# The last rotary pass of latent attention heads on 32 rows in four row groups, with two key pieces side by side

## The chip, the core and the metric

The kernel runs on one core of one Trainium2 chip. The metric is the time of one execution in device microseconds. Before the change it was 594.4 us (median of three runs, 593.88 to 594.96). Single-precision products are made of matmuls in a rounded single-precision type, three for one exact product: high part by high part, low by high and high by low.

## The reference

One decoder block: 512 tokens and 16 learned leading tokens (528 keys), width 1024. From one projection of the normalised input come two attention branches of 16 heads each. The latent branch (MLA) has queries and keys of 64 plain and 32 rotary features; the rotary key is one for all heads. The other branch (FoX) adds a cumulative forget gate to the scores and has no rotary part.

```python
k_pe = rope(k_pe_raw, pos)[:, None]
q_m = jnp.concatenate([q_nope, rope(q_pe, pos)], axis=-1)
k_m = jnp.concatenate([k_nope, jnp.broadcast_to(k_pe, (B, MLA_HEADS, L, MLA_ROPE_DIM))], axis=-1)
o_mla = causal_block_attention(q_m, k_m, v_mla, MLA_SCALE)
y_mla = (o_mla * jax.nn.silu(z_mla)) @ w_br_mla[l]
...
o_fox = causal_block_attention(fox_heads(fq), fox_heads(fk), fox_heads(fv), FOX_SCALE, cum)
y_fox = (o_fox * jax.nn.silu(z_fox)) @ w_br_fox[l]
mixed = (jax.nn.sigmoid(gate_a) * y_mla + jax.nn.sigmoid(gate_b) * y_fox) @ w_out[l]
h = h + rmsnorm(mixed, post_norm_g[l])
```

## The kernel before

The kernel has a preparation (norm, transposes, latent projections), an attention part of sixteen stages and a merge of the branches. A stage is one branch and one pair of heads; FoX and MLA alternate, so there are eight MLA stages. In the attention part the order of TensorE's instructions is the order of the program text (`manual_schedule`); the other engines and SP's queue of DMAs are ordered by a scheduler. Between the parts of a stage stand "fills": projections for the next stage (`fq`, `fk`, `v`, `z`, `mq`, `mk`) and for gates (`pg`), full 128-row matmuls that need nothing of the running softmax.

A stage begins with `scores(0)`: the query tiles 0, 1 and 2 (128 queries each) against the 144, 272 and 400 keys that they may see. Tile 0 and tile 1 share a PSUM bank, tile 2 has its own; there is one such set for each head of the pair, four banks in all (pool `stp`, names `st`). Then come the products with the values of the stage before (`ov`, function `values`), then `scores(1)`: tile 3 against all 528 keys, in pieces of 272 and 256 keys, in the same four banks again. VectorE takes the scores out of the banks (L783), ScalarE makes the exponentials, and SP turns the probabilities with DMA transposes (`pt<-pn`), which the `ov` products of the next stage read.

Each piece of an MLA stage takes five passes, and each pass two matmuls, one per head, on partitions 0 to 63 and 64 to 127. Such a pair runs side by side in two halves of the array's rows. Three passes are the plain features (`hlk,hlq`). Two are the rotary ones: the tile `QP` holds, for each head, the high part of the rotary query on 32 partitions and its low part on the next 32. `KP[0]` (shown as KPH) holds the high part of the rotary key four times, on each group of 32 partitions, so one pass makes high by high and low by high. `KP[1]` (KPL) holds the key's low part at partitions 0 and 64, and zeros (L231) on the 32 partitions behind each, so the last pass of 64 rows makes high by low. These five are listed in `sets` (L737) and issued in `scores` (L761). A run of three rows in the timeline, hlk, KPH and KPL, is one piece.

`QP` is filled by DMA: for the first pair of heads from SBUF in `rest` (L643), for later pairs from a DRAM tile in `load_qp` (L570). The copies of the rotary key are made once, ahead of the stages (L916 to L918).

Of the kernel before, what the change touches and what calls it, by code (L numbers as in the profile page):

```python
# [23 lines left out]
S = 512  # L24
# [25 lines left out]
def f32(ap):  # L50
    return ap.bitcast(F32)
# [3 lines left out]
def block_kernel(ctx: ExitStack, tc: tile.TileContext, x, meta_tokens, pre_norm_g, w_in, fox_forget_b,  # L55
# [40 lines left out]
    def mm(*a, **k):  # L96
        nc.tensor.matmul(*a, **k)  # L97
# [441 lines left out]
    with ExitStack() as att:  # L539
# [6 lines left out]

        cb = [[thp.tile([128, L], F32, tag="th", name=f"cb{n}{h}") for h in range(2)] for n in "pm"]
        QP = ac.tile([128, S], F32R, tag="QP", name="QP")
        maskt = ac.tile([128, L + 16], BF16, tag="maskt", name="maskt")
        nc.gpsimd.memset(maskt, 0.0)  # L550
        nc.gpsimd.affine_select(out=maskt[:, 400:L], in_=maskt[:, 400:L], pattern=[[-1, 128]], base=0,
# [17 lines left out]

        def load_qp(pr):  # L570
            dma(f32(QP), qpe_dram[2 * pr : 2 * pr + 2].rearrange("h i x f s -> (h i x f) s"))

        def q_mla(pr):
            ld = []
# [30 lines left out]
        def pe_unit(g):  # L605
# [37 lines left out]
            def rest(x):  # L643

                tt, rr = room()[1], results(x)
                with nullcontext() if g else tc.issue_after(masks[0]):
                    nc.gpsimd.tensor_tensor(out=tt[:, x], in0=tt[:, x], in1=tt[:, 3 - x], op=(ALU.subtract, ALU.add)[x])
                hi, lo = rr[:, 0], rr[:, 1]
                nc.gpsimd.tensor_copy(hi.bitcast(F32R), tt[:, x])
                split_lo(nc.gpsimd, lo.bitcast(F32R), tt[:, x], hi)  # L650
                if g:
                    store(x, 0, 8)
                else:

# [75 lines left out]
        def attention(br, pr):  # L730
# [30 lines left out]
            def scores(g):  # L761

                banks = (((0, 0, 144, 0), (1, 0, 272, 144)), ((2, 0, 400, 0),)) if g == 0 else \
                    (((3, 0, HALF, 0),), ((3, HALF, L - HALF, 0),))

                def fn():
# [3 lines left out]
                    sfs[g] = aw.tile([128, 2, (2 * SF_STEP + 400, L)[g]], F32, tag=f"sf{g}", name=f"sf{nm_}{g}", bufs=1)  # L770
                    for ib, parts in enumerate(banks):
                        ps = [stp.tile([128, 512], F32, tag="st", name=f"st{nm_}{g}{ib}{h}") for h in range(2)]
                        for b, c0, w, o in parts:
# [3 lines left out]
                        for b, c0, w, o in parts:  # L777
                            for h in range(2):
                                nb = sums["nb"][:, h, b : b + 1]
                                for a, e, in1 in added(h, b, c0, c0 + w):  # L780

                                    with tc.high_priority(offset=100):
                                        nc.vector.tensor_tensor_reduce(  # L783
                                            out=sf_of(h, b)[:, a:e], in0=ps[h][:, o + a - c0 : o + e - c0],
                                            in1=in1, scale=-scale, scalar=3.0e38 if a == 0 else nb,
                                            op0=ALU.add, op1=ALU.min, accum_out=nb)
# [528 lines left out]
```

## Time and profile before

| | before |
|---|---|
| median of three runs | 594.4 us |
| the profiled execution | 594.59 us |
| its span, first to last instruction | 592.5 us |
| granted TensorE clock, mean | 0.998 |
| TensorE matmul busy | 584.1 us, 3841 matmuls |
| of these, rotary passes of the MLA stages | 160 (80 with KPH, 80 with KPL) |
| VectorE, ScalarE, GpSimd busy | 412.3, 357.8, 200.3 us |

All numbers but the median come from one profiled execution. PE is TensorE's matmuls, PEld its weight loads, DVE VectorE, ACT ScalarE, POOL GpSimd, SPq the queue of SyncE that issues DMAs. A form such as 64*128 64x272 is a matmul with weights of 64 rows by 128 columns and 272 moving columns. In a timeline equal instructions that follow each other stand in one row with a count. Matmuls are pipelined and the ends of their rows are modelled: the distance between starts tells the pace.

### The profile page before, as it was taken

How to read it: one execution, taken by the hardware profiler on the slowest of the kernel's cores; microseconds unless marked ns; L12 is line 12 of the kernel's file. 1: busy time of each engine (PE TensorE's matmuls, PEld its weight loads, DVE VectorE, ACT ScalarE, POOL GpSimd, SP SyncE). 2: the span in 40 equal slices, each digit the busy share in tenths (PEclk: the TensorE clock that was granted, in tenths of full speed). 3: DMA queues.
4: the chain of work that ended last, by engine and by line, in shares of the span. 5: the costliest groups of instructions: out<-in, count | busy, mean ns of one | idle time of the engine just before them, and what ended most of it. 6: DMA issues, size and time to landing. Idle time of an engine off the chain costs nothing.

```text
span 592.5 us, 11129 instructions
## 1 busy us (share of the span) xinstructions
PE 584.1 (99%) x3841; PEld 501.0 (85%) x3841; DVE 412.3 (70%) x1155; ACT 357.8 (60%) x816; POOL 200.3 (34%) x271
## 2 busy tenths in 40 slices
PE   8999999999999999999999999999999999999996
PEld 6989789889889888888898897888998998888884
DVE  5854876775775776766758748797647777468957
ACT  7846775784774784766748748764444363433753
POOL 4317746455358463553544544420000000000000
PEclk9999999999999999999999999999999999999999
DMA  8535599999995998896895986866822534333603
GB/s 288 119 87 161 124 176 239 230 201 225 168 201 116 229 211 217 188 188 175 177 207 147 203 160 146 193 137 216 273 72 71 143 95 132 94 106 108 213 2 142
DMA packets 220001, 97.47 MB, mean 165 GB/s; under 512 B 131457, under 2 KB 209673, under 8 KB 219945
## 3 DMA queue, kind: packets, MB, share of 16 engines
q1 hardware_dynamic: 219944, 96.77, 69.4%
q8 instruction: 30, 0.49, 0.3%
q14 instruction: 27, 0.21, 0.1%
HBM read 62.36 MB, written 3.97 MB: 112 GB/s over the span
## 4 chain that ended last, share of the span: by engine, by line
PE 97%; DMA 1%; SPq 0%; DVE 0%; issue 0%; POOL 0%; DVEq 0%; ACT 0%; POOLq 0%
PE z L97 19%; PE pg L97 15%; PE v L97 9%; PE st L97 8%; PE fk L97 8%; PE fq L97 8%; PE x L97 8%; PE py L97 7%; PE ov L97 5%; PE psm L97 4%; PE y L97 2%; PE mq L97 2%; PE mk L97 1%; DMA wsr<-in_w_in_dram 1%; PE ppe L97 1%; PE pt L100 1%
## 5 line engine op out<-in xcount | busy, mean ns | idle before, releaser
L103 POOL TENSOR_TENSOR wl<-wraw,wh 128x1024 fp32r<-128x1024 f32 (+2 forms) x62 | 120.2, 1947 | 96.3 <-ACT wh L130 73.9
L130 ACT CAST wh<-wraw 128x1024 fp32r<-128x1024 f32 (+1 forms) x72 | 74.6, 1040 | 53.5 <-PE py L97 16.8
L791 ACT ACTIVATE sf<-sf,nb 128x272 f32<-128x272 f32 (+3 forms) x128 | 72.5, 568 | 17.1 <-DVE nb L783 15.6
L819 DVE SCALAR_TENSOR_TENSOR pn<-sf,ri,pn 128x128 f16<-128x128 f32 (+3 forms) x128 | 68.7, 576 | 7.3 <-ACT pn L818 7.1
L103 DVE TENSOR_TENSOR wl<-wraw,wh 128x512 fp32r<-128x512 f32 (+1 forms) x54 | 51.0, 947 | 27.5 <-ACT wh L1052 18.9
L818 ACT ACTIVATE pn<-sf,ri 128x128 f16<-128x128 f32 (+3 forms) x128 | 61.2, 550 | 9.9 <-ACT sf L791 7.9
L97 PE MATMUL z<-uTh,wh 128*128 128x512 f32 x128 | 51.0, 398 | 0.0
L97 PE MATMUL pg<-uTh,wh 128*128 128x512 f32 x128 | 50.3, 393 | 0.0
L97 PE MATMUL z<-uTl,wh 128*128 128x512 f32 x128 | 50.1, 391 | 0.0
L97 PE MATMUL z<-uTh,wl 128*128 128x512 f32 x128 | 50.0, 391 | 0.0
L97 PE MATMUL pg<-uTl,wh 128*128 128x512 f32 x128 | 49.9, 390 | 0.0
L97 PE MATMUL pg<-uTh,wl 128*128 128x512 f32 x128 | 49.9, 390 | 0.0
L97 PE MATMUL st<-hlk,hlq 64*128 64x272 f32 (+3 forms) x480 | 45.5, 308 | 0.0
L1052 ACT CAST wh<-wraw 128x512 fp32r<-128x512 f32 x28 | 17.3, 619 | 39.8 <-DVE wraw L1061 15.4
L687 DVE TENSOR_REDUCE vsc<-v 128x1 f32<-128x272 f32 (+1 forms) x32 | 13.2, 433 | 39.9 <-PE v L97 39.9
L97 PEld LDWEIGHTS st<-hlk,hlq 64*128 64x128 f32 x480 | 34.6, 185 | 6.0 <-ACT vh L706 2.8
L97 PE MATMUL v<-uTh,wl 128*128 128x256 f32 (+1 forms) x128 | 36.5, 285 | 0.0
L97 PE MATMUL fk<-uTl,wh 128*128 128x256 f32 (+1 forms) x128 | 36.5, 285 | 0.0
L97 PE MATMUL fk<-uTh,wh 128*128 128x256 f32 (+1 forms) x128 | 36.5, 285 | 0.0
L97 PE MATMUL v<-uTl,wh 128*128 128x256 f32 (+1 forms) x128 | 36.5, 285 | 0.0
L97 PE MATMUL fk<-uTh,wl 128*128 128x256 f32 (+1 forms) x128 | 36.4, 285 | 0.0
L97 PE MATMUL v<-uTh,wh 128*128 128x256 f32 (+1 forms) x128 | 36.4, 285 | 0.0
(285 smaller groups left out, 1615.4 us busy)
## 6 DMA issues: line engine op xcount, KB each, us to landing
wraw<-in_w_in_dram SPq DMA_DIRECT2D x56, 512.0 KB, 4.5
cbp<-c_dram SPq DMA_DIRECT2D x16, 264.0 KB, 4.5
wraw<-in_w_br_fox_dram SPq DMA_DIRECT2D x8, 512.0 KB, 4.4
tb<-in_w_out_dram SPq DMA_DIRECT2D x8, 512.0 KB, 5.2
wraw<-in_w_br_mla_dram SPq DMA_DIRECT2D x8, 512.0 KB, 4.1
wraw<-in_w_out_dram SPq DMA_DIRECT2D x6, 512.0 KB, 3.6
xr<-in_x_dram SPq DMA_DIRECT2D x4, 512.0 KB
out_dram<-yo SPq DMA_DIRECT2D x8, 256.0 KB, 2.0
```

The source lines that it names most:

```text
L97: nc.tensor.matmul(*a, **k)
L100: nc.tensor.transpose(*a)
L103: return eng.tensor_tensor(out=lo, in0=src, in1=f32(hi), op=ALU.subtract)
L130: nc.scalar.copy(wh[:, :n], raw[:, :n])
L687: nc.vector.tensor_reduce(out=sc[:, i : i + 1], in_=ps, op=ALU.max, axis=AX.X, apply_absolute_value=True)
L791: exps[g] = nc.scalar.activation(sf, sf, AF.Exp, bias=sums["nb"][:, h, b : b + 1], scale=-1.0, accum_out=sums["su"][:, h, b : b + 1]).ins
L818: normed[:] = [nc.scalar.activation(hi, sf, AF.Copy, scale=rib).ins]
L819: nc.vector.scalar_tensor_tensor(out=lo, in0=sf, scalar=rib, in1=hi, op0=ALU.mult, op1=ALU.subtract)
L1052: nc.scalar.copy(to[0], src)
```

## The change

The low rotary pass of the MLA stages uses 32 rows instead of 64: the high part of the rotary query against the low part of the rotary key, without the rows of zeros. The low part of the key is copied to all four groups of 32 partitions. A new tile `Q2` holds the high part of the rotary query a second time, for the upper 256 queries, on the second 32 partitions of each head (partitions 32 to 63 and 96 to 127). With it a second piece of a head can be taken on other rows of the array than the first. The low passes are collected in a list and issued by `own`; the place in the list tells whether a piece reads `QP` or `Q2`. The scores of MLA are evicted once all pieces of a group are complete; FoX is evicted as before.

```diff
+        Q2 = ac.tile([128, S // 2], F32R, tag="Q2", name="Q2")
...
         def load_qp(pr):
             dma(f32(QP), qpe_dram[2 * pr : 2 * pr + 2].rearrange("h i x f s -> (h i x f) s"))
+            for h in range(2):
+                dma(f32(Q2[64 * h + 32 : 64 * h + 64]), qpe_dram[2 * pr + h, 0, :, :, S // 2 :].rearrange("x f s -> (x f) s"))
...
                             dma(f32(QP[r : r + 16]), rr[16 * h : 16 * h + 16, i])
+                        r = 64 * h + 32 + 16 * x
+                        dma(f32(Q2[r : r + 16]), rr[16 * h : 16 * h + 16, 0, S // 2 :])
...
-                return out + [(QP[hs, qs], KP[i][hs, ks]) for i in range(2)]
+                return out + [(QP[hs, qs], KP[0][hs, ks])]
+
+            def low_rotary(h, b, c0, w, moved):
+                rs = slice(64 * h + 32 * moved, 64 * h + 32 * moved + 32)
+                q_ = Q2[rs, 128 * (b - 2) : 128 * (b - 2) + 128] if moved else QP[rs, 128 * b : 128 * b + 128]
+                return q_, KP[1][rs, c0 : c0 + w]
...
-            last_set = (4, 2)[br]
+            last_set = (3, 2)[br]
...
+                def own(late_):
+                    for n, (ps, b, c0, w, o) in enumerate(late_):
+                        for h in range(2):
+                            mm(ps[h][:, o : o + w], *low_rotary(h, b, c0, w, n), start=False, stop=True, skip_group_check=True)
+                    late_.clear()
...
                         for b, c0, w, o in parts:
                             for i, ops in enumerate(zip(*(sets(h, b, c0, w) for h in range(2)))):
                                 for h, (Q, K) in enumerate(ops):
-                                    mm(ps[h][:, o : o + w], Q, K, start=(i == 0), stop=(i == last_set))
...
+                                    mm(ps[h][:, o : o + w], Q, K, start=(i == 0), stop=(br == 1 and i == last_set),
+                                       skip_group_check=not br)
+                            if not br:
+                                late_.append((ps, b, c0, w, o))
+                                if len(late_) == 1 and g == 0:
+                                    own(late_)
+                        if br:
+                            evict(ps, parts)
+                    if not br:
+                        own(late_)
+                        for ps, parts in zip(pss, banks):
+                            evict(ps, parts)
...
-        nc.sync.dma_start(f32(KP[1][64 : 64 + ROPE]), f32(KP[1][0:ROPE]))
+        for r in (64, 32, 96):
+            nc.sync.dma_start(f32(KP[1][r : r + ROPE]), f32(KP[1][0:ROPE]))
```

TensorE, second group of scores (tile 3) of the first MLA stage, before; st_1202 and st_1203 are the banks of the first piece for the two heads, st_1216 and st_1217 those of the second:

```order
L97 MATMUL st_1203<-KPH,QP 128x272
L97 MATMUL st_1202<-KPL,QP 128x272
L97 MATMUL st_1203<-KPL,QP 128x272
L97 MATMUL st_1216<-hlk_1074,hlq_1055 128x256
...
L97 MATMUL st_1217<-KPH,QP 128x256
L97 MATMUL st_1216<-KPL,QP 128x256
L97 MATMUL st_1217<-KPL,QP 128x256
L97 MATMUL fq_1243<-uTh,wh_1237 128x512
```

The same place in the changed program; the four banks are st_1209, st_1210, st_1219 and st_1220, and Q_710 is the tile Q2:

```order
L97 MATMUL st_1210<-KPH,QP 128x272
L97 MATMUL st_1219<-hlk_1081,hlq_1062 128x256
...
L97 MATMUL st_1220<-KPH,QP 128x256
L97 MATMUL st_1209<-KPL,QP 128x272
L97 MATMUL st_1210<-KPL,QP 128x272
L97 MATMUL st_1219<-KPL,Q_710 128x256
L97 MATMUL st_1220<-KPL,Q_710 128x256
L97 MATMUL fq_1250<-uTh,wh_1244 128x512
```

The two KPL rows of the first piece moved behind the second piece and stand beside its own; the number of matmuls is the same.

TensorE, first group (tiles 0, 1, 2) of the same stage in the changed program; 1134 and 1135 are the banks that tiles 0 and 1 share, 1156 and 1157 those of tile 2:

```order
L97 MATMUL st_1135<-KPH,QP 128x144
L97 MATMUL st_1134<-KPL,QP 128x144
L97 MATMUL st_1135<-KPL,QP 128x144
L97 MATMUL st_1134<-hlk_1081,hlq_1062 128x272
...
L97 MATMUL st_1135<-KPH,QP 128x272
L97 MATMUL st_1134<-KPL,QP 128x272
L97 MATMUL st_1135<-KPL,QP 128x272
L97 MATMUL st_1156<-hlk_1081,hlq_1062 128x400
```

Here no row moved: `own` is called after each piece, and each KPL pair, now of 32 rows, stands where it stood before.

SP's queue, DMAs for the first pair of heads, before:

```order
L91 DMA_TRANSPOSE vp_720<-vh 128x9x128
L91 DMA QP<-gT_778 16x512 x4
L91 DMA QP<-gT_779 16x512 x4
L851 DMA cbp_705<-c_dram 128x528
L851 DMA cbp_706<-c_dram 128x528
L91 DMA_TRANSPOSE pt<-pn_715 128x6x128
```

And in the changed program:

```order
L91 DMA_TRANSPOSE vp_721<-vh 128x9x128
L91 DMA QP<-gT_781 16x512 x2
L91 DMA Q_710<-gT_781 16x256
L91 DMA QP<-gT_781 16x512 x2
L91 DMA Q_710<-gT_781 16x256
L91 DMA QP<-gT_782 16x512 x2
L91 DMA Q_710<-gT_782 16x256
L91 DMA QP<-gT_782 16x512 x2
L91 DMA Q_710<-gT_782 16x256
L882 DMA cbp_705<-c_dram 128x528
```

Four small DMAs more stand ahead of the bias loads and of the transposes of the first stage's probabilities.

More of the change, by code (lines that the diff above doesn't have):

```diff
@@ L764, in scores, with evict @@
                     (((3, 0, HALF, 0),), ((3, HALF, L - HALF, 0),))
+                def own(late_):
[3 more added lines that the diff above has]
+                    late_.clear()
+                def evict(ps, parts):
+                    for b, c0, w, o in parts:
+                        for h in range(2):
+                            nb = sums["nb"][:, h, b : b + 1]
+                            for a, e, in1 in added(h, b, c0, c0 + w):
+                                with tc.high_priority(offset=100):
+                                    nc.vector.tensor_tensor_reduce(
+                                        out=sf_of(h, b)[:, a:e], in0=ps[h][:, o + a - c0 : o + e - c0],
+                                        in1=in1, scale=-scale, scalar=3.0e38 if a == 0 else nb,
+                                        op0=ALU.add, op1=ALU.min, accum_out=nb)
                 def fn():
@@ L770, in fn @@
                     sfs[g] = aw.tile([128, 2, (2 * SF_STEP + 400, L)[g]], F32, tag=f"sf{g}", name=f"sf{nm_}{g}", bufs=1)
+                    pss, late_ = [], []
                     for ib, parts in enumerate(banks):
                         ps = [stp.tile([128, 512], F32, tag="st", name=f"st{nm_}{g}{ib}{h}") for h in range(2)]
+                        pss.append(ps)
                         for b, c0, w, o in parts:
@@ L775, in fn @@
                                 for h, (Q, K) in enumerate(ops):
-                                    mm(ps[h][:, o : o + w], Q, K, start=(i == 0), stop=(i == last_set))
[L777 to L786, printed above, removed]
+                                    mm(ps[h][:, o : o + w], Q, K, start=(i == 0), stop=(br == 1 and i == last_set),
[10 more added lines that the diff above has]
+                            evict(ps, parts)
                     with tc.high_priority(offset=60):
```

## The prediction

> **What bounds the kernel now.** I read the page first, then the waits of the matrix engine, then its timeline through one latent stage.
>
> ```profile
> span 592.5 us, 11129 instructions
> PE 584.1 (99%) x3841; PEld 501.0 (85%) x3841; DVE 412.3 (70%) x1155; ACT 357.8 (60%) x816; POOL 200.3 (34%) x271
> PE 97%; DMA 1%; SPq 0%; DVE 0%; issue 0%; POOL 0%; DVEq 0%; ACT 0%; POOLq 0%
> PE spun L97 <- DVE KPL L231: 1.5, 1, 1.5
> PE psm L97 <- POOL wsh L298: 1.1, 1, 1.1
> ```
>
> TensorE (PE) is busy for 99% of the span, the chain that ended last runs over it for 97%, and its only two waits lie before the attention begins. So the order and the spacing of its own matmuls set the time: whatever the latent stages lose or gain there goes into the end one for one, unless a new wait is made. The timeline of the first latent stage, one row for each run of matmuls with one pair of operands, columns start, length, shape, count:
>
> ```profile
> 78.75 0.39 PE L97 MATMUL z<-uTh,wl 128*128 128x512 f32 x1
> 79.07 0.56 PE L97 MATMUL st<-hlk,hlq 64*128 64x144 f32 x6
> 79.47 0.28 PE L97 MATMUL st<-KPH,QP 64*128 64x144 f32 x2
> 79.58 0.28 PE L97 MATMUL st<-KPL,QP 64*128 64x144 f32 x2
> 79.69 0.59 PE L97 MATMUL st<-hlk,hlq 64*128 64x272 f32 x6
> 80.11 0.29 PE L97 MATMUL st<-KPH,QP 64*128 64x272 f32 x2
> 80.24 0.29 PE L97 MATMUL st<-KPL,QP 64*128 64x272 f32 x2
> 80.36 0.71 PE L97 MATMUL st<-hlk,hlq 64*128 64x400 f32 x6
> 80.91 0.34 PE L97 MATMUL st<-KPH,QP 64*128 64x400 f32 x2
> 81.09 0.34 PE L97 MATMUL st<-KPL,QP 64*128 64x400 f32 x2
> 81.37 2.04 PE L97 MATMUL ov<-pt,vp 80*64 80x512 f16 x26
> 83.82 0.29 PE L97 MATMUL st<-KPH,QP 64*128 64x272 f32 x2
> 83.94 0.29 PE L97 MATMUL st<-KPL,QP 64*128 64x272 f32 x2
> 84.07 0.51 PE L97 MATMUL st<-hlk,hlq 64*128 64x256 f32 x6
> 84.42 0.28 PE L97 MATMUL st<-KPH,QP 64*128 64x256 f32 x2
> 84.53 0.28 PE L97 MATMUL st<-KPL,QP 64*128 64x256 f32 x2
> 84.75 0.50 PE L97 MATMUL fq<-uTh,wh 128*128 128x512 f32 x1
> 85.08 0.40 PE L97 MATMUL fq<-uTl,wh 128*128 128x512 f32 x1
> 85.32 0.40 PE L97 MATMUL fq<-uTh,wl 128*128 128x512 f32 x1
> ```
>
> Lengths overlap, so the price of a pair (two heads, x2) is the distance between starts. 144 keys: 79.58 to 79.69, 0.11 us. 272: 80.24 to 80.36, 0.125 (two differences of 0.13 and 0.12). 400: 80.91 to 81.09, 0.18. 256: 84.42 to 84.53, 0.115. The last rotary pass, KPL, thus costs 0.11 + 0.125 + 0.18 in the first group and 0.125 + 0.115 in the second.
>
> What else is to be seen is where the row count before the star changes. The last 64-row pair starts at 84.53; at its own pace the first 128-row fq would follow at 84.645 and the second, 0.235 later (85.08 to 85.32 is 0.24), at 84.88. It starts at 85.08: **a change of row count costs 0.20**. Into the stage: z at 78.75 plus 0.235 plus three pairs of 0.11 gives 79.315 for KPH; it is at 79.47, 0.155 late. With 144 keys the pace is not that of the columns but of something else, so less is lost. By columns (0.055 between 272 and 400, 0.43 ns each) a 144 piece streams in 0.06, and 0.05 of its 0.11 is hidden in the change: 0.155 to 0.16 against 0.205.
>
> Is 32 rows such a change? No row of before goes from 64 to 32. The nearest is a detour from 128 rows to two 16-row transposes and back, and beside it a change of the column count alone:
>
> ```profile
> 33.05 0.35 PE L97 MATMUL psm<-wsl,uTh 128*128 128x432 f32 x1
> 33.33 0.26 PE L100 MATMUL pc<-ident,sm 16*128 16x16 f32 x2
> 33.52 0.46 PE L97 MATMUL psm<-wsh,uTh 128*128 128x432 f32 x1
> 33.82 0.36 PE L97 MATMUL psm<-wsh,uTl 128*128 128x432 f32 x1
> 34.02 0.36 PE L97 MATMUL psm<-wsl,uTh 128*128 128x432 f32 x1
> 33.33 0.16 PEld L100 LDWEIGHTS pc<-ident,sm 16*128 16x128 f32 x2 [0.29 <-ACT sm L413]
> 24.39 0.60 PE L100 MATMUL pc<-ident,sm 128*128 128x128 f32 x4
> 24.83 0.71 PE L100 MATMUL pt<-ident,hn 128*128 128x128 f32 x5
> ```
>
> At the pace of 0.20 (33.82 to 34.02) psm would stand at 33.25 and 33.45; the second stands at 33.82. The detour cost 0.37, of which the two tiny transposes can be 0.2 at most: 0.09 to 0.19 for each of its two changes, and the weight load before it lay idle for 0.29. The four transposes at 24.39, whose last has 48 columns instead of 128 at unchanged rows, take 4 x 0.11 to the next at 24.83: that change is free.
>
> **The change part by part.** *First group (tiles 0, 1, 2).* In the built order the list of open pieces is emptied after each piece, since it holds one each time, so nothing is paired here. Each of the three KPL pairs stays in its place and only goes from 64 rows to 32. No column is saved. Added are five changes of row count: into and out of the 144 pair, into and out of the 272 pair, and into the 400 pair; the way out of that one to ov existed before. Two at 0.16 beside the 144 piece, three at 0.205: 0.32 + 0.615 = 0.935.
>
> *Second group (tile 3).* Here two pairs become four matmuls in four row groups: 0.125 is saved, and as the last of the stage is now 272 wide and not 256, 0.006 is given back. One change is added, from the 256-key KPH pair into the four: 0.205. Sum +0.086.
>
> *A stage:* 0.935 + 0.086 = 1.02; eight latent stages: **8.2 us**. Bounds of the unmeasured 64-to-32 change: nothing, as the free column change (then only the saving is left, -0.12 x 8 = -0.95), and 0.25, a quarter over the dearest that the rows show (6 x 0.25 - 0.12 is 1.38 a stage, 11.0). I take the 64-to-128 price, since every change of row count in these rows pays and the detour shows that it holds for 16 rows as well. That four loads and four streams run side by side is not shown either: if they went two by two, the saving of 0.12 is gone, +1.0 in all.
>
> The Trainium skill (TensorEngine Tiling, Tiling Modes, key properties) says that changing the tiling mode, as against the tile, drains the TensorE, and lists 64 and 32 rows as different modes; by it all six changes pay, which no row here shows for 64 to 32. The same skill (TensorE: Matmul & The Clock Gate, Packing small matmuls) gives 3.07 times for four 32-row tiles and not 4; by an estimate from that page the four would cost 1.3 of one, and the sum would rise by 8 x 0.04 = 0.3.
>
> *Evictions, now after all pieces.* The second group reuses the first group's banks.
>
> ```profile
> L783 DVE CUSTOM_DVE_ANT_0 sf<-st,maskt x64: 302/434/571, 80.7 to 381.8; 128x272 f32<-128x272 f32 x32, 128x144 f32<-128x144 f32 x16, 128x400 f32<-128x400 f32 x16
> ```
>
> The 400 pair would end at about 81.09 + 0.34 + 0.94 = 82.4, and two evictions of 0.57 free its banks at 83.5. The second group begins behind ov, at 81.37 + 2.04 = 83.4 now and 84.3 then, and takes those banks half a microsecond later. Cover is over a microsecond; nothing is charged. The softmax of the stage starts up to 1 us later, but so does all TensorE work behind it.
>
> *DMAs.* SP issues two more copies of the low key (at 45 us, long before 79.6), four more for the first pair and two for each later pair.
>
> ```profile
> 61.95 6.11 SPq L91 DMA_DIRECT2D QP<-gT  x8
> L91 SPq DMA_DIRECT2D QP<-gT x8: 507/582/587, 62.0 to 67.5; - x8
> 69.31 9.34 SPq L91 DMA_TRANSPOSE pt<-pn  x4
> 75.19 3.46 SPq L91 DMA_TRANSPOSE pt<-pn  x1
> 97.33 4.01 SPq L91 DMA_TRANSPOSE pt<-pn  x1
> DMA to landing us min/median/max: 2.7/4.2/5.5
> 103.55 0.84 PE L97 MATMUL ov<-pt,vp 80*64 80x512 f16 x6
> ```
>
> An issue takes 0.58, 0.6 with what lies between, so the transposes of the probabilities behind the four start up to 2.4 late. The fourth, at 75.19, lands by the median at 79.4, by the longest at 80.7; its reader ov moves from 81.37 to 82.3. Slack 1.6 to 2.9 against 2.4. A stage on, the one at 97.33 lands by 102.8 at the latest; its reader moves from 103.55 to 104.6: slack 1.8 or more, if the queue hasn't caught up by then. Cost 0 to 0.8, taken as 0.1. Were the cover gone, the whole 2.4 would be TensorE wait. Copies for later pairs go in behind or among transposes of latent stages, 1 us each at most.
>
> **The sum.** 8.2 + 0.1 on the profiled execution's 594.59 (span 592.5 and 2.1 around it) is 602.9. The median of the runs shown, 594.4, is 0.2 lower: I predict **602.7**.
>
> **The rivals.** *Changing between 64 and 32 rows is free* (the same two heads keep their halves of the array, only fewer rows are used). For it: the free column change, and the KPL rows' strict pace of 0.11, which shows that a new weight load normally runs ahead of its turn. Against it: both kinds of row change in the rows. Then the first group is unchanged, the second saves 0.12, 594.4 - 0.95 + 0.1 gives 593.5: not slower. It decides below 0.02 per change, where 6 x 0.02 eats the 0.12. The Trainium skill (TensorE: Matmul & The Clock Gate, Packing small matmuls) has loads pulled ahead of running matmuls when row groups don't conflict; it would speak for this rival, but here the 32 rows lie inside the 64 just used.
>
> *The engine stops but the load runs ahead,* so that a change costs about half, 0.1 in place of 0.205 and 0.06 in place of 0.16. That is 2 x 0.06 + 4 x 0.1 - 0.12 = 0.4 a stage, 597.7. For it: the detour's lower figure of 0.09. Against: the loads idle for 0.29 before it.
>
> *SP's queue becomes a wait as well.* All of the forecast, and the first two ov wait for late transposes: up to the full 2.4, less than half of it covered, say 1.5 more, 604.2, and 605 with the dearer change. For it: SP's rows above fill 62 to 68 and 69.3 to 78.7 us. Against: both slacks above.
>
> **How the numbers follow.** Forecast 0.74 (601.5 to 603.9), SP's wait 0.11, half price 0.07, free change 0.08. The range runs from 600.0 to 605.2: it leaves out the free and the half-price change, 0.15, and little above. About 0.2%, 1.2 us, is what a measurement here tells from no change. Of the free change's 0.08, 0.03 lies below 593.2 and 0.05 within; 0.01 more within comes from prices just above free. So faster 0.03, same 0.06, slower 0.91.
>
> **What would show it.** In the first latent stage of the changed kernel, the distance from each KPH pair to the KPL pair behind it: 0.27 to 0.39 instead of 0.11 to 0.18, with weight loads idle before each; scores of the first group 0.94 longer; in the second group four KPL rows within 0.02 us, then fq. No new TensorE wait on st or pt. The forecast is wrong if KPL follows KPH at 0.11 to 0.18, if the four come in two steps, or if an ov row waits for a transpose.

## The result and the profile after

The changed kernel takes 603.91 us (median of five runs, 603.07 to 606.26), the kernel before, beside it on the same chip, 594.81 (five runs, 593.88 to 594.96). The ratio is 1.0169, 95% interval 1.0154 to 1.0183: 9.1 us slower, where 602.7 was predicted, 8.3 more than the 594.4 known then. The profiled execution is the shortest of the five, 603.07; the others are 0.5 to 3.2 us longer.

The page of the changed kernel, and the waits of TensorE in it (columns: total us, times, longest):

```profile
span 601.0 us, 11165 instructions
PE 592.5 (99%) x3841; PEld 503.0 (84%) x3841; DVE 415.0 (69%) x1155; ACT 357.9 (60%) x816; POOL 199.7 (33%) x271
PE spun L97 <- DVE KPL L231: 1.4, 1, 1.4
PE psm L97 <- POOL wsh L298: 0.4, 1, 0.4
PE v L97 <- DVE hlq L103: 0.3, 1, 0.3
```

As many matmuls as before, TensorE still 99% busy, and 8.5 us more of span. PE's busy time is 8.4 us longer (592.5 against 584.1), so the loss stands in the page as busy time, and the page by itself doesn't tell where it is. One wait is new, `v` on VectorE's `hlq`; it is neither on `st` nor on `pt`. The first latent stage in the timeline of the changed kernel:

```profile
79.08 0.28 PE L97 MATMUL st<-KPH,QP 64*128 64x144 f32 x2
79.28 0.34 PE L97 MATMUL st<-KPL,QP 32*128 32x144 f32 x2
79.55 0.64 PE L97 MATMUL st<-hlk,hlq 64*128 64x272 f32 x6
80.03 0.29 PE L97 MATMUL st<-KPH,QP 64*128 64x272 f32 x2
80.25 0.39 PE L97 MATMUL st<-KPL,QP 32*128 32x272 f32 x2
80.57 0.82 PE L97 MATMUL st<-hlk,hlq 64*128 64x400 f32 x6
81.22 0.34 PE L97 MATMUL st<-KPH,QP 64*128 64x400 f32 x2
81.50 0.45 PE L97 MATMUL st<-KPL,QP 32*128 32x400 f32 x2
82.04 2.04 PE L97 MATMUL ov<-pt,vp 80*64 80x512 f16 x26
...
84.97 0.28 PE L97 MATMUL st<-KPH,QP 64*128 64x256 f32 x2
85.19 0.39 PE L97 MATMUL st<-KPL,QP 32*128 32x272 f32 x2
85.19 0.38 PE L97 MATMUL st<-KPL,Q 32*128 32x256 f32 x2
85.51 0.50 PE L97 MATMUL fq<-uTh,wh 128*128 128x512 f32 x1
81.50 0.18 PEld L97 LDWEIGHTS st<-KPL,QP 32*128 32x128 f32 x2 [0.27 <-issue]
```

Put it beside the stage of before. KPH to KPL: 0.20, 0.22 and 0.28 here, 0.11, 0.13 and 0.18 there, so 0.09 or 0.10 more ahead of each 32-row pair. KPL to the next piece: 0.27 and 0.32 against 0.11 and 0.12, 0.16 to 0.20 more behind it. The `hlk` row behind grows as well, 0.64 against 0.59 and 0.82 against 0.71: a part of the way back to 64 rows falls one pair later. The weight load of KPL, which ran ahead before, idles for 0.27. In the second group all four KPL matmuls start at 85.19.

The cleanest measure of a stage is the distance of the first `fq` behind it from that of the next latent stage, deep in the attention, where nothing waits. Sixth and seventh latent stage, the kernel before:

```profile
296.67 0.50 PE L97 MATMUL fq<-uTh,wh 128*128 128x512 f32 x1
338.53 0.50 PE L97 MATMUL fq<-uTh,wh 128*128 128x512 f32 x1
```

and the changed kernel:

```profile
302.93 0.50 PE L97 MATMUL fq<-uTh,wh 128*128 128x512 f32 x1
345.75 0.50 PE L97 MATMUL fq<-uTh,wh 128*128 128x512 f32 x1
```

41.86 against 42.82: a stage is 0.96 longer. Over all eight, with small differences from one to the next, the starts of TensorE's matmuls move by 7.8 us. The other 0.7 of the profiled execution: 0.16 before the first `ov` (from KPH of tile 2 to `ov` it is 0.82 here and 0.66 in the seven later stages, 0.46 in all eight of before), 0.6 at `v` in the first latent stage, 0.3 behind the last matmul, and 0.4 less at the beginning, where the waits for the first weights differ from one execution to the next.

### The profile page after: what moved, and what is told of

Same layout as the page of the kernel before. It is cut to its first block, busy times and chain, and to the rows that moved or that the text cites. A ratio compares the mean times of both kernels' runs of the same rounds, so it can differ in the third digit from the quotient of the medians.

```text
span 601.0 us, 11165 instructions
## 1 busy us (share of the span) xinstructions
PE 592.5 (99%) x3841; PEld 503.0 (84%) x3841; DVE 415.0 (69%) x1155; ACT 357.9 (60%) x816; POOL 199.7 (33%) x271
## 4 chain that ended last, share of the span: by engine, by line
PE 83%; DVE 1%; ACT 0%; issue 0%; DVEq 0%
PE z L97 17%; PE pg L97 14%; PE st L97 8%; PE x L97 8%; PE py L97 7%; PE v L97 7%; PE fk L97 6%; PE fq L97 6%; PE ov L97 5%; PE y L97 2%; PE mq L97 2%; PE mk L97 1%; PE ppe L97 0%; DVE pn L850 0%; DVE yo L1255 0%
## 5 line engine op out<-in xcount | busy, mean ns | idle before, releaser
L850 DVE SCALAR_TENSOR_TENSOR pn<-sf,ri,pn 128x128 f16<-128x128 f32 (+3 forms) x128 | 70.6, 591 | 7.5 <-ACT pn L849 7.3
```

The source lines that it names most:

```text
L850: nc.vector.scalar_tensor_tensor(out=lo, in0=sf, scalar=rib, in1=hi, op0=ALU.mult, op1=ALU.subtract)
```

## The experiments

The rivals were: a change of row count is dear (the forecast), cheap, or the loss comes from DMAs and waits. A fourth was put down with the first runs: not the changes cost time but each group of 32-row matmuls by itself, 0.27. Four kernels vary the number of changes, two undo the pairing, five take the change's side effects one by one, and one takes away changes that the kernel before has. For all: median of a kernel's runs, the median of the kernel before in the same batch (594.3 to 594.6), and the ratio's interval. "Stage" is the distance of the two `fq` rows above in the kernel's own trace, less 41.86; "beside" is what the median has gained beyond eight stages. The other distances between latent stages, where no stop falls into them, agree with the table within 0.07 (one piece: 0.24 to 0.27).

| kernel | changes of row count added a stage | stage | 8 stages | median less before | beside |
|---|---|---|---|---|---|
| one piece on 32 rows | 1 | +0.20 | 1.6 | +1.8 | 0.2 |
| all pieces on 32 rows in place | 8 | +1.53 | 12.2 | +11.8 | -0.4 |
| the change | 6 | +0.96 | 7.7 | +9.1 | 1.4 |
| the change without Q2 | 6 | +1.06 | 8.5 | +9.3 | 0.8 |
| the change, Q2 not read | 6 | +1.08 | 8.6 | +12.2 | 3.6 |
| tiles 1 and 2 side by side too | 4 | +0.46 | 3.7 | +7.1 | 3.4 |
| tile 0 on 64 rows as well | 2 | +0.12 | 1.0 | +5.2 | 4.2 |
| the change, first Q2 DMAs later | 6 | +0.97 | 7.8 | +9.8 | 2.0 |
| 64 rows, Q2 not read | 0 | -0.03 | -0.2 | +8.0 | 8.2 |
| 64 rows, Q2 read | 0 | -0.03 | -0.2 | +2.6 | 2.8 |
| 64 rows, no Q2 | 0 | -0.03 | -0.2 | +1.9 | 2.1 |
| 64 rows, no Q2, nothing held back | 0 | -0.02 | -0.2 | +0.9 | 1.1 |

**1. The price alone.** The kernel before, all low passes on 32 rows in place, no second query tile:

```diff
-                return out + [(QP[hs, qs], KP[i][hs, ks]) for i in range(2)]
+                rs = slice(64 * h, 64 * h + 32)
+                return out + [(QP[hs, qs], KP[0][hs, ks]), (QP[rs, qs], KP[1][rs, ks])]
```

> The kernel before, with nothing but its low passes on 32 rows, each in its place: no Q2, no late eviction, no pairing. Changes of row count added: five in the first group and three in the second, eight a stage. Theory: 0.90 + 3 x 0.205 = 1.5 a stage, 12.1 in all, 606.9 us. Rival (late evictions and DMAs): 594.8. Rival (each 32-row group of matmuls costs p by itself, with 4 p - 0.12 = 0.975 from the changed kernel, p = 0.27): 5 x 0.27 x 8 = 10.9, 605.7.

Measured: 606.21 us (606.09 to 606.28, four runs), ratio 1.0196 (1.018 to 1.0211). Work taken away (half the rows of every low pass) and nothing else done costs 11.8 us. In its trace no `ov` and no `v` waits. The way into and out of a pair in the second group:

```profile
84.19 0.29 PE L97 MATMUL st<-KPH,QP 64*128 64x272 f32 x2
84.41 0.39 PE L97 MATMUL st<-KPL,QP 32*128 32x272 f32 x2
84.73 0.62 PE L97 MATMUL st<-hlk,hlq 64*128 64x256 f32 x6
```

0.22 and 0.32, as in the changed kernel, where before had 0.12 and 0.13. The free change and the DMA rival fall: there is no new DMA and no new place here. Between the theory (606.9) and the price for each 32-row group (605.7) the median doesn't decide; the stage, 1.53, is that of the theory (12.1 / 8 = 1.51) rather than that of the group (10.9 / 8 = 1.36).

**2. One change.** The same, for tile 2 only, whose 400-key pair stands ahead of `ov`, so that one change is added:

```diff
+                rs = slice(64 * h, 64 * h + 32) if b == 2 else hs
+                return out + [(QP[hs, qs], KP[0][hs, ks]), (QP[rs, qs], KP[1][rs, ks])]
```

> The kernel before, with only tile 2's low pass (400 keys) on 32 rows, in its place in front of ov: one change of row count a stage is added, 64 to 32; the way out to 128 rows replaces the one from 64. Theory: 0.205 x 8 = 1.6, 596.4 us, and KPL starts 0.28 behind the 32-row pair's 64-row neighbour's own stream, ov no later behind KPL than before. Rival (free change): 594.8. Rival (p = 0.27 per 32-row group): 597.0.

596.24 us (595.75 to 596.83, ten runs), ratio 1.0028 (1.0019 to 1.0038). Tile 2 in the first latent stage:

```profile
80.36 0.34 PE L97 MATMUL st<-KPH,QP 64*128 64x400 f32 x2
80.64 0.45 PE L97 MATMUL st<-KPL,QP 32*128 32x400 f32 x2
81.02 2.04 PE L97 MATMUL ov<-pt,vp 80*64 80x512 f16 x26
```

From KPH to `ov` it is 0.66, where before had 0.46 (80.91 to 81.37), half of the 0.20 more ahead of the 32-row pair and half behind it. `ov` is later by 0.199 or 0.198 in each of the eight stages. One change of row count is 0.20, and eight in place (two of them at a short 144 piece) are 1.53: the price goes with the number of changes. The half price (0.1) falls, and so does 0.27 for each group of 32-row matmuls, which would stand here in full.

**3. What the pairing brings.** The changed kernel, but the four KPL matmuls of the second group on the same rows, so two pairs one behind the other; Q2 is filled and not read:

```diff
-                            mm(ps[h][:, o : o + w], *low_rotary(h, b, c0, w, n), start=False, stop=True, skip_group_check=True)
+                            mm(ps[h][:, o : o + w], *low_rotary(h, b, c0, w, 0), start=False, stop=True, skip_group_check=True)
```

> The changed kernel, with the second group's two low pieces both from QP, one behind the other on the same 32 rows, instead of side by side (Q2 is loaded and not read). The number of changes of row count is that of the changed kernel. Theory: the second pair starts 0.11 to 0.13 behind the first, with no new stop, so 0.12 x 8 = 1.0 over the changed kernel, about 604.9 us where that one has 603.9. Rival (each 32-row group costs 0.27 whatever stands before it): the second pair 0.27 behind the first, 2.2 over, 606.1.

606.64 us (605.34 to 607.13, four runs), ratio 1.0206 (1.0189 to 1.0223). The stage says what was asked: 1.08 against 0.96, so side by side is worth 0.12 a stage, 1.0 us in all. The second pair starts 0.23 behind the first and not 0.11 to 0.13, which by itself looks like the price for each 32-row group (0.27). But the 0.1 more is the half that a change into 32 rows leaves behind it (experiment 2), and it isn't paid again: `fq` follows 0.44 behind the first pair, 0.12 later than behind the four, and the stage is longer by 0.12 and not by 0.27. As for the median: the scheduler put the loads of a tile that nobody reads earlier into SP's queue (those of the second pair ahead of the transposes at 91.91, where the changed kernel has them at 102.95, behind); `ov` waits for transposes three times (1.7 us). So the median holds two effects. The same without the tile and its DMAs (the diff shows the rows alone):

```diff
...
-                rs = slice(64 * h + 32 * moved, 64 * h + 32 * moved + 32)
-                q_ = Q2[rs, 128 * (b - 2) : 128 * (b - 2) + 128] if moved else QP[rs, 128 * b : 128 * b + 128]
-                return q_, KP[1][rs, c0 : c0 + w]
+                rs = slice(64 * h, 64 * h + 32)
+                return QP[rs, 128 * b : 128 * b + 128], KP[1][rs, c0 : c0 + w]
```

> The changed kernel without Q2: no DMA of it, the second group's two low pieces one behind the other on 32 rows of QP. Six changes of row count a stage stay, late evictions stay. Both theories: 594.5 + 8 x (0.975 + 0.12) = 603.2 us, 0.6 more if v waits in the first latent stage. Theory 2 adds: runs within half a microsecond of each other and no ov that waits for pt, against 606.6 for the same matmuls with the DMAs. Theory 1 (DMAs are harmless): the same time as that run, 606.6.

603.63 us (603.5 to 603.72, four runs), ratio 1.0153 (1.0138 to 1.0168): no slower than the change itself. What the pairing saves, the DMAs that it needs take back.

**4. Fewer changes.** First the list is kept open over tiles 1 and 2, so that these, too, stand side by side:

```diff
-                                if len(late_) == 1 and g == 0:
+                                if b == 0:
                                     own(late_)
```

> The changed kernel with the list emptied early only behind tile 0, so that the low pieces of tiles 1 and 2 stand side by side (272 and 400 keys, QP and Q2) as those of tile 3 do. Four changes of row count a stage: into and out of tile 0's pair, into tiles 1 and 2's four, into tile 3's four. Theory 1: 2 x 0.16 + 0.205 - 0.125 = 0.40 in the first group, 0.08 in the second, 3.8 us in all, and 1.6 to 2.6 of side effects as in the 64-row runs without and with Q2: 600 to 601. Rival (pairing brings the time back): 595 or less.

601.66 us (600.06 to 602.86, four runs), ratio 1.0119 (1.0095 to 1.0143): 0.7 above the upper end of what was expected. The stage came as worked out: four changes, two of them at 0.155, less two pairings of 0.12, make 0.47; measured 0.46. Then tile 0 keeps its 64-row pass (which adds a product of low by low that the kernel before leaves out), and two changes are left:

```diff
-                return out + [(QP[hs, qs], KP[0][hs, ks])]
+                return out + [(QP[hs, qs], KP[i][hs, ks]) for i in range(1 if b else 2)]
...
-                            if not br:
+                            if not br and b:
                                 late_.append((ps, b, c0, w, o))
-                                if len(late_) == 1 and g == 0:
-                                    own(late_)
```

> The cheapest form of the idea: tile 0's low pass on 64 rows in its place (it then adds low by low), tiles 1 and 2 side by side on 32 rows, tile 3 side by side. Two changes of row count a stage, 250 keys' worth of pairs saved: (0.205 - 0.125) + 0.08 = 0.16 a stage, 1.3 us, and 1.6 to 2.6 of side effects: 597.2 to 598.2. Rival (with the pairing complete, the saving outweighs the changes): below 594.

599.82 us (598.16 to 600.8, four runs), ratio 1.0089 (1.0069 to 1.0108), 1.6 above the upper end expected. Here too the stage is near (+0.12, where 0.16 was expected) and the rest is not. The first group in it, and its waits:

```profile
80.17 0.35 PE L97 MATMUL st<-KPH,QP 64*128 64x400 f32 x2
80.45 0.39 PE L97 MATMUL st<-KPL,QP 32*128 32x272 f32 x2
80.45 0.44 PE L97 MATMUL st<-KPL,Q 32*128 32x400 f32 x2
82.20 2.04 PE L97 MATMUL ov<-pt,vp 80*64 80x512 f16 x26 [1.30 <-DMA pt<-pn]
PE ov L97 <- DMA pt<-pn: 3.5, 2, 2.2
```

At this first `ov` SP's order is still that of the changed kernel, and the earlier TensorE comes, the longer it waits for the transposes: its `ov` starts at 82.20, the changed kernel's at 82.04. What was taken out of the matmuls is given back at the next DMA. The second wait (2.2 at 106.73, and 1.6 at 107.07 in the kernel of four changes) is no such plain case: tile 2 now reads Q2, and the scheduler put the loads of QP and Q2 ahead of that stage's transposes, whose first is issued at 93.66 and not at 89.21. How much of the wait this order makes isn't separated. Even with the cheapest form of the idea two changes (0.40) cost more than two pairings save (0.24).

**5. The side effects without the changes.** The changed kernel with low passes on 64 rows of `QP` (adding low by low), Q2 loaded and not read:

```diff
-                rs = slice(64 * h + 32 * moved, 64 * h + 32 * moved + 32)
-                q_ = Q2[rs, 128 * (b - 2) : 128 * (b - 2) + 128] if moved else QP[rs, 128 * b : 128 * b + 128]
-                return q_, KP[1][rs, c0 : c0 + w]
+                rs = slice(64 * h, 64 * h + 64)
+                return QP[rs, 128 * b : 128 * b + 128], KP[1][rs, c0 : c0 + w]
```

> All of the change but the row count: the low passes are collected, evicted late and all DMAs of Q2 are made, yet each low pass takes 64 rows of QP again (Q2 is loaded and not read; since the low key now lies on all four groups, the pass adds low by low). Theory (the six changes of row count a stage carry the loss, 0.975 us a stage in the trace of the changed kernel): only the side effects are left, about 0.16 us of wait before the first ov and up to 0.6 before v in the first latent stage, 595 to 596 us. Rival (late evictions and the extra DMAs carry it): 602 or more. Rival (a 32-row matmul is slow by itself): 595 to 596, as the theory.

602.44 us (601.32 to 604.21, four runs), ratio 1.0135 (1.0111 to 1.016). By its number my theory falls; its trace tells why it was no test of it. The stages are not longer than before, and `ov` waits for 7.6 us in four places. From the second pair of heads on, SP's queue holds loads of the unread tile that wait for stores, ahead of transposes:

```profile
PE ov L97 <- DMA pt<-pn: 7.6, 4, 2.9
90.73 1.63 SPq L91 DMA_DIRECT2D Q<-qpe_dram  x2
92.46 1.23 SPq L91 DMA_TRANSPOSE pt<-pn  x1
```

The longest wait, 2.9 at the first `ov`, stands ahead of that, where SP's order is the changed kernel's; the order can explain the other three, 4.7 in all. So the same with Q2 read, on 64 rows, its other partitions zero, and SP's order exactly that of the changed kernel:

```diff
+        for h in range(2):
+            nc.vector.memset(f32(Q2[64 * h : 64 * h + 32]), 0.0)
...
-                rs = slice(64 * h + 32 * moved, 64 * h + 32 * moved + 32)
+                rs = slice(64 * h, 64 * h + 64)
```

> The changed kernel with its low passes on 64 rows and with Q2 read: the first 32 partitions of each head in Q2 are zeros, so tile 3's second piece takes 64 rows of Q2, and the pass from QP adds low by low. SP's queue has the same DMAs in the same order as in the changed kernel, which was not so in the first 64-row run, where the unread Q2 was loaded earlier and stood in the queue waiting for the stores. No change of row count is added. Theory 1 (the row changes carry the whole loss): 595 to 596 us. Theory 2 (the DMAs of Q2 make the transposes late by some 2 us, and the longer matmul streams of the changed kernel hid most of that): ov waits for pt in the first stages, 597 to 601 us, spread over a microsecond or more.

596.93 us (596.73 to 597.15, five runs), ratio 1.0041 (1.0027 to 1.0055): between the two ranges, next to the lower end of the second, and the runs lie within 0.4 us, where the second had a spread of a microsecond or more. With 64 rows in place of 32, 6.5 us of the 9.1 are gone. What is left are waits:

```profile
PE ov L97 <- DMA pt<-pn: 1.2, 1, 1.2
PE ov L97 <- PE st L97: 0.7, 1, 0.7
```

Without Q2 and its DMAs, still on 64 rows (low by low added), only the order of passes and evictions and two key copies are left of the change. The edit is that of the kernel without Q2 in experiment 3, with `rs = slice(64 * h, 64 * h + 64)`:

> The changed kernel with 64-row low passes (adding low by low) and without Q2: what is left is the collecting of the low pass of tile 3's first piece, the late evictions with VectorE's changed order, and two more copies of the low key. Both theories: 594.5 to 595.3 us, the upper end if v waits for the accumulator in the first latent stage. Rival (late evictions carry a part of the loss): 596 or more.

596.15 us (595.86 to 597.1, six runs), ratio 1.0031 (1.002 to 1.0043). A miss, and the rival's range: 1.9 us that I had charged nothing for. Its matmuls stand still at `v` in the first latent stage (0.9), at another `v` at 180 us (0.3) and at a gate product at 410 us (0.5). The Q2 DMAs add 0.8 to it (596.93 less 596.15). Last, the 272-key piece of the second group is completed at once again:

```diff
-                                if len(late_) == 1 and g == 0:
+                                if len(late_) == 1:
                                     own(late_)
```

> The kernel with 64-row low passes and without the second query tile (it measured 596.15 us, 1.7 above the kernel before; as there, each low pass adds a product of low by low that the kernel before leaves out), with one thing undone: in the second group, too, each piece's low pass stands right behind the piece, so that the 272-key piece is complete 0.5 us earlier. The evictions stay behind all pieces of their group in the program text, and the two more key copies stay. With it VectorE's order around the second group is again that of the kernel before. Theory 1: the 1.7 us come from holding the 272 piece's last pass back, which puts VectorE's evictions of the second group behind more products of the probabilities and its later work with them: 594.4 to 595.2, and no wait at v. Theory 2: they come from evictions that stand behind all pieces or from the key copies: 595.8 to 596.5, as before.

595.13 us (594.59 to 595.82, eleven runs), ratio 1.0013 (1.0004 to 1.0022): theory 1, at its upper end; the interval still excludes no loss. Holding one pass back costs 1.0 us. That it does so by way of VectorE is read from what two of the stops waited for (`hlq` at `v`, `wl` at the gate product, both VectorE's); no run shows it by itself. The later stops are gone; at `v` in the first latent stage there are still some 0.8 in several steps, though VectorE's order is again that of before. There ScalarE is late:

```profile
89.93 1.05 ACT L130 CAST wh<-wraw 128x1024 fp32r<-128x1024 f32 x1 [2.68 <-DMA wraw<-in_w_in_dram]
90.88 0.73 ACT L816 ACTIVATE sf<-sf,nb 128x528 f32<-128x528 f32 x1
```

In the kernel before, that cast stood at 87.47 and the exponentials behind it at 89.28. The block of weights was issued at the same place of the same queue and landed later; why, stays open. The cast is as late in the other two kernels that are the change without Q2 (89.44 on 64 rows, 89.90 on 32) and not in the changed kernel (87.58), so the 0.9 at this `v` can't be put down to the held-back pass alone.

**6. DMAs put later.** The changed kernel, the first pair's four Q2 DMAs behind the first stage's transposes:

```diff
-                        r = 64 * h + 32 + 16 * x
-                        dma(f32(Q2[r : r + 16]), rr[16 * h : 16 * h + 16, 0, S // 2 :])
...
+                for x in range(2):
+                    for h in range(2):
+                        r = 64 * h + 32 + 16 * x
+                        dma(f32(Q2[r : r + 16]), gT[x][16 * h : 16 * h + 16, 4, S // 2 :])
```

> The changed kernel with the first pair's four DMAs of Q2 behind the first stage's transposes of probabilities instead of in front of them. Theory 2: the first ov no longer waits; median 602.5 to 603.3 us where the changed kernel had 603.9. Theory 1: 603.9 as before.

604.13 us (603.06 to 605.45, four runs), ratio 1.0162 (1.0146 to 1.0179): a miss, 0.8 above the range expected. The first `ov` no longer waits; the one of the next stage does:

```profile
97.42 0.39 PE L97 MATMUL v<-uTh,wh 128*128 128x256 f32 x1 [0.71 <-DVE hlq L103]
106.35 2.04 PE L97 MATMUL ov<-pt,vp 80*64 80x512 f16 x26 [1.47 <-issue]
```

No releaser is named for that `ov`; SP issued two transposes of probabilities from 97.90 to 104.29, the last work of its queue that this `ov` reads. So I read it as the same wait, one stage on: what the four issues cost isn't saved by moving them behind one stage's transposes, since the next stage's come behind them.

**7. The other way round: changes taken away.** If a change of row count costs 0.20, then the kernel before pays for its own. From the second stage on, `scores(1)` directly behind `scores(0)`, values behind both; the first piece of `scores(1)` takes two of the fills' three accumulator banks:

```diff
-                        ps = [stp.tile([128, 512], F32, tag="st", name=f"st{nm_}{g}{ib}{h}") for h in range(2)]
+                        ps = [acc(f"sa{nm_}{h}") if g and not ib else stp.tile([128, 512], F32, tag="st", name=f"st{nm_}{g}{ib}{h}")
+                              for h in range(2)]
...
-            for fn in [s0] + late:
-                fn()
+            s0()
...
             s1()
+            for fn in late:
+                fn()
```

> The kernel before, with 64-row low passes and no Q2, but from the second stage on the second group of scores directly behind the first and the values of the stage before behind both, so that two of the four changes of row count that every stage has fall away (ov to st at 0.205 and st to the fill at 0.205; st to ov stays, ov to the fill is 128 rows on both sides). The first piece of the second group takes two of the fills' three accumulator banks, since the first group's banks are not yet free. Theory 1: 15 stages x 0.41 = 6.1 us less, 588.3 where nothing waits, up to 594 where scores wait for banks or fills for accumulators. Rival (the stops are hidden or moved by the waits for banks): 594.5 or more.

601.84 us (600.33 to 603.0, four runs), ratio 1.0124 (1.0104 to 1.0144): the rival's range. Of the two changes that were to fall away one did not. The expectation took `ov` to the fill for free, since both have 128 rows there; the first latent stage shows otherwise:

```profile
83.06 2.04 PE L97 MATMUL ov<-pt,vp 80*64 80x512 f16 x26
85.02 0.50 PE L97 MATMUL fq<-uTh,wh 128*128 128x512 f32 x1
85.36 0.40 PE L97 MATMUL fq<-uTl,wh 128*128 128x512 f32 x1
85.61 0.40 PE L97 MATMUL fq<-uTh,wl 128*128 128x512 f32 x1
```

The second `fq` stands 0.34 behind the first, as it does behind the 64-row pairs of the kernel before, and not 0.24; and `fq` starts 0.15 behind the last pair of `ov`, where those pairs follow each other at 0.056. Together that is 0.20, and it is there behind all sixteen `ov`. From the last `z` ahead of the scores to this `fq` the stage takes 5.99 (79.03 to 85.02), 6.00 before (78.75 to 84.75): nothing is saved. The other 0.20 is lost again in the last piece, whose two heads run a pass apart here: from its first `hlk` (82.18) to `ov` it is 0.88, and 0.68 to `fq` before (84.07 to 84.75). And waits came:

```profile
PE st L97 <- DVE nb L784: 4.5, 7, 0.6
PE v L97 <- POOL wl L103: 2.0, 1, 2.0
```

Without `ov` between them the two groups of scores meet at the same banks in the FoX stages, which VectorE hasn't emptied yet. With 0.9 more at `psm` in the preparation (2.0 against 1.1, ahead of anything that this edit moves) these waits are 7.4 of the 8.4 us that the profiled execution is longer. No version here beats the kernel before.

## Why the prediction was right, and where it was not

**TensorE bounds, one for one: right.** TensorE is 99% busy after, and the 7.8 us that its stages grew arrive at the end.

**The price of a change: right.** 0.205 was put from a 64-to-128 change; 64 to 32 costs 0.20 (experiment 2). The first group was put at 0.935 and the second at 0.086, a stage at 1.02; the stage measures 0.96. In place of 8.2 us, 7.8 came. Where the price would be seen was put wrong in size: 0.27 to 0.39 from KPH to KPL was expected, 0.20 to 0.28 is there, because about half of it shows behind the 32-row pair (experiment 2) and, on the way out, a little one pair further. By this distance alone the half price would have been read, which gives 0.17 to 0.28; the stage tells them apart, 0.96 against its 0.4. The page of the Trainium skill (TensorEngine Tiling, Tiling Modes, key properties) says that a change of mode drains the TensorE, and has 64 and 32 rows as different modes; these rows agree in that each change costs 0.20, and what happens in the array meanwhile they don't show.

**Four side by side: right.** The four start within 0.01, and `fq` follows 0.32 behind the first of them (85.19 to 85.51), as it follows 0.31 behind the single 256 pair of experiment 1 (85.40 to 85.71). The 1.3 that I estimated from the Trainium skill (TensorE: Matmul & The Clock Gate, Packing small matmuls), 0.04 a stage, isn't seen. Nor do the loads run ahead of the change: that of KPL comes after an idle 0.27. That section of the Trainium skill has loads pulled ahead when row groups don't conflict, and here the 32 rows lie inside the 64 just used.

**"Nothing is charged" for the evictions: wrong.** This step failed. I had looked at whether TensorE would find its score banks free, and it does; no `st` waits. What I hadn't looked at is the queue of VectorE. Before, its order around the second group was:

```profile
85.50 0.73 DVE L819 SCALAR_TENSOR_TENSOR pn<-sf,ri,pn 128x128 f16<-128x128 f32 x2 [0.20 <-ACT pn L818]
86.15 0.43 DVE L783 CUSTOM_DVE_ANT_0 sf<-st,maskt 128x272 f32<-128x272 f32 x1
...
94.85 0.68 DVE L103 TENSOR_TENSOR hlq<-fq,hlq 128x512 fp32r<-128x512 f32 x1
```

and in the changed kernel:

```profile
85.61 5.80 DVE L850 SCALAR_TENSOR_TENSOR pn<-sf,ri,pn 128x128 f16<-128x128 f32 x4 [0.20 <-ACT pn L849]
91.34 0.43 DVE L789 CUSTOM_DVE_ANT_0 sf<-st,maskt 128x272 f32<-128x272 f32 x1
...
96.76 0.69 DVE L103 TENSOR_TENSOR hlq<-fq,hlq 128x512 fp32r<-128x512 f32 x1
97.50 0.38 PE L97 MATMUL v<-uTh,wh 128*128 128x256 f32 x1 [0.34 <-DVE hlq L103]
```

The last pass of the 272-key piece stands at 85.19 in place of 83.94, and two more products of the probabilities stand ahead of its eviction (a row's shape is that of its first instruction; the two have 256 columns). They run while GpSimd makes its weight products:

```profile
86.15 4.99 POOL L103 TENSOR_TENSOR wl<-wraw,wh 128x1024 fp32r<-128x1024 f32 x2
```

and the four take 5.80 us. The evictions start 5.2 us later, the exponentials 3.4 (92.64 against 89.28 on ScalarE), `hlq` 1.9, and `v`, which the program text puts there, stands 0.6. On 64 rows and without Q2, undoing the order is worth 1.0 us (experiment 5, last), but there at later stops; at this `v` some 0.8 stayed, with ScalarE late. So the 0.6 rests on the rows of the changed kernel.

**DMAs, 0 to 0.8 taken as 0.1: the upper end.** The Q2 DMAs cost 0.8 between the two 64-row kernels, and 0.6 on 32 rows by the column "beside" (1.4 against 0.8 without Q2). In the profiled execution the first `ov` waits 0.16 (for the transposes, as I take it; so short a stop has no releaser in the list), so the slack was about what I had worked out, but I had counted late transposes as a case by itself. They come and go with the execution: the change's runs spread over 3.2 us, those of experiments 1 and "without Q2" over 0.2. That it is these DMAs that spread them is not shown: the 64-row kernel that has them too spread over 0.4, and kernels without them over 1.1 (one piece) and 1.2 (the other two on 64 rows without Q2).

**The sum.** 8.2 + 0.1 was predicted on the median, 7.8 + 1.3 came. An error of 0.4 in the large term and one of 1.2 in the small ones partly cancel. That is luck as far as the small terms go; the large one stands by itself, and 603.9 lies inside 600.0 to 605.2.

**The rivals.** Free change: fell at the first stage (KPL 0.09 later, load idle). Half price: fell, 0.20 a change. SP's queue as a wait: 0.16 in the profiled execution where 1.5 was put, but real in kind, as 2.3 and 3.5 us where TensorE stops less. An `ov` that waits for a transpose was one of the prediction's own signs of being wrong; the 0.16 is a small case of it.

## What to carry to other kernels

Rows of the array that were saved were worth nothing by themselves here (in experiment 1 the price of its eight changes, 1.51, is all of the 1.53), and each change of row count between matmuls was paid for, 0.2 us: count the changes before the rows, and narrow a pass only if it can stand beside others often enough to save more than its way in and out. When a result is completed later, look not only at whether its buffer is free in time, but at what the scheduler will put ahead of its reader on that reader's engine. A saving on the bound engine is worth its full size only as far as the next DMA that it meets: two of these kernels gained 0.50 and 0.84 us a stage against the change, 4.0 and 6.7 in all, and came out 2.0 and 3.9 shorter (each against the kernel before in its batch), with new waits for transposes, a part of which goes with another order of SP's queue.

## What the runs showed of the hardware

- 64 to 32 rows, within the same half of the array and for the same two heads, costs as much as 64 to 128: 0.20 us a change (0.155 to 0.16 beside a 144-column piece). A change of the weights' column count alone was free among single transposes in the trace of before (one with 48 columns among others with 128). But from `ov` to a fill 0.20 is paid with 128 rows on both sides (experiment 7, and once in the kernel before, at 401.66): there pairs with 64-column weights in f16, started within 0.004 of each other, give way to single matmuls with 128 columns in f32. Whether the pairing of columns or the number type does it, no run here separates.
- The price of going in and out doesn't lie in one place: some 0.09 ahead of the first narrow matmul and 0.16 to 0.20 behind the pair, with 0.05 to 0.11 more inside the following six matmuls.
- Four 32-row matmuls of 272 and 256 columns in four row groups start within 0.01 us and take no longer than one pair of them (the next matmul 0.32 behind the four, 0.31 behind one pair of 256 columns).
- VectorE's four products of the probabilities took 5.80 us in the changed kernel, beside two weight products of GpSimd, and 3.67 in the 64-row kernel without Q2, where only one ran beside them (there the second waited for its weights):

```profile
85.09 3.67 DVE L844 SCALAR_TENSOR_TENSOR pn<-sf,ri,pn 128x128 f16<-128x128 f32 x4 [0.21 <-ACT pn L843]
85.63 2.44 POOL L103 TENSOR_TENSOR wl<-wraw,wh 128x1024 fp32r<-128x1024 f32 x1
```

In both, the two products of 256 columns are the ones that grow: 2.58 and 2.61 in the changed kernel, both beside GpSimd, 2.58 and 0.47 here, where only the first is. The other thirty of that shape take 0.47 to 0.54 in the changed kernel and 0.47 to 0.49 in the kernel before, whose two beside GpSimd take 1.91 and 1.82. So the length of one engine's work depends on what the other does at that time, and the same order cost the one kernel two microseconds more than the other.
